# Convolution rows of the last group in five buffers stored from GpSimd's queue, sample loads behind head loads, softmax rows in other places

## The chip, the cores and the metric

The kernel runs on one core of a Trainium2 chip. The core has five engines, each with its own instruction order: TensorE (PE; PEld is its weight load), VectorE (DVE), ScalarE (ACT), GpSimd (POOL) and SyncE (SP). Here SP only issues DMAs, and GpSimd issues some beside its arithmetic. The metric is the device time of one execution in microseconds, as the median of several runs. Before the change it was 2948.85 us (three runs, 2946.77 to 2949.27).

## The reference

One layer of a streaming encoder for 2048 prompt frames and 8 samples of 16 new frames, all in fp32. What concerns this change is the first sub-layer, the mixer:

```
proj = rmsnorm(x) @ w_in               # -> q | k | v | u_val | u_gate
s    = q @ k^T / 8 + bias              # 8 heads of 64, each query sees 9 chunks of 64 keys
att  = softmax(s) @ v                  # samples: 256 cached keys and values and their own 16
u    = u_val * sigmoid(u_gate)
c    = silu(layernorm(causal_depthwise_conv(u, width 31)))
y    = concat(att, c) @ w_out
```

Cross-attention into 256 memory tokens and a SwiGLU layer follow; new key, value and convolution caches are outputs as well.

## The kernel before

The prompt is 16 tiles of 128 frames, and the samples together are a 17th tile (`S_TILE`). Every fp32 product is three matmuls of high and low parts (L283 to L285, L291). The phases follow each other: memory keys (`phase_mem`), the input projection with the convolution (`phase_proj`), attention, the output projection (`mixout`), cross-attention, SwiGLU.

`phase_proj` runs over three groups of six, six and five tiles. Per group it makes `u`, the values, then keys and queries, whose high and low parts go to DRAM (`ks`, `qs`, L714). The convolution of a group runs beside the projection on VectorE (L523) and GpSimd (L533). Its result `ct` is normalised by `conv_norm`, tile by tile: transposes (L538), statistics (L540), the normalised rows `xn` (L546), transposes back (L550), then on ScalarE `z` (L553, four activations) and its tanh (L556), on VectorE their product (L557), and a DMA that stores `z` into `cs[t]` (L558). For the first two groups this is spread over the next group. For the last group the five tiles' steps (`behind`, L731) stand between the last projections and attention. `z` has two buffers, and the store is issued by SP.

`attention` goes through 128 units (8 heads of 16 tiles). A unit makes scores (L865), a row minimum on VectorE (L802) and an exponential on ScalarE (L804) into a softmax row `z` (also so called, but another tag, with eight places); four units later come transposes (L882) and their split by a ScalarE cast (L883) and a VectorE subtraction (L884); every four units the value product (L895), a copy (L899) and a sum (L901). A head's keys, queries and values come back from DRAM by `head_load` (L789, L790) into two sets of buffers, during the head before; head 1's during the end of the projection. Beside head h runs `sample(h)`, whose loads are cached keys `kt` (L809), cached values `vc` (L811) and new values `vn` (L813); its scores are L825. The bias rows `bs` (L908) are loaded once.

`mixout` starts with the sample tile. It loads `cs[t]` (L1008) and splits it (L1023, L1024).

What sets the order: a scheduler places the recorded instructions on each engine in the order of their recording, except where one is free to go earlier; `issue_after(x)` keeps what is recorded under it behind `x`. Each engine runs its instructions strictly in that order. Buffers are places in a few large arenas (`sbF`, `fa`, `fb`, `sbR`; offsets in KB), given out in rotation by tag; an instruction waits for whoever used the same bytes before. `fb` from 0 holds `ct`; `fa` from 4 to 8 holds the two `z`.

Of the kernel before, what the change touches and what calls it, by code (L numbers as in the profile page):

```python
# [17 lines left out]
P = 128  # L18
# [118 lines left out]
class Build:  # L137
# [22 lines left out]
    def early(self, ctx):  # L160
# [15 lines left out]
                   .lay(sbR, 56, ("hhz", 8, 1), ("hlz", 8, 1))  # L176
                   .lay(sbR, 104, ("vv", 2, 2)))
        smp = Region().lay(fa, 28, ("qsamp", 2, 1), ("ksamp", 2, 1))
# [268 lines left out]
    def phase_proj(self):  # L447
# [87 lines left out]
        def conv_norm(t, cts, off, tag="tr"):  # L535
# [13 lines left out]
            for j in range(4):  # L549
                nc.tensor.transpose(pz[:, j, :], xn[:, j, :], self.ident[:, :])  # L550
            z = self.t(pool, [P, 4, P], F32, "z", 2)
            for j in range(4):
# [4 lines left out]
            nc.vector.scalar_tensor_tensor(z[:, :, :], th[:, :, :], 1.0, z[:, :, :], ALU.add, ALU.mult)  # L557
            nc.sync.dma_start(self.cs[t], z[:, :, :].rearrange("p a b -> p (a b)"))  # L558

# [17 lines left out]
        for gi, subs in enumerate(GROUPS):  # L577
# [100 lines left out]
            def qk(which, j, blk, x):  # L678
# [14 lines left out]
                else:  # L693
# [4 lines left out]
                    for i, t in enumerate(sub):  # L698
# [13 lines left out]
                        else:  # L712
                            nc.sync.dma_start(A["new_att_k_prompt"][(t - 12) * P:(t - 11) * P, :], kos[t][:, :])
                nc.sync.dma_start(dst[:, :, col:col + npc].rearrange("c p n -> p c n"),  # L714
                                  sp[:, :, :npc].bitcast(F32))

# [41 lines left out]
    def att_pools(self):  # L758
        sbF, sbR, fa, fb = self.sbF, self.sbR, self.fa, self.fb
        self.attp = (Region().lay(sbF, 34.5, ("kt", 4.25, 2), ("pp", 1.5, 1), ("vn", 2, 2))  # L760
                     .at("z", 2.5, (fa, [24]), (fb, [0, 2.5, 5]), (fa, [9, 11.5, 14, 16.5]))
                     .lay(fb, 7.5, ("vc", 4, 2), ("nmx", 0.03125, 12), ("sm", 0.03125, 2))
                     .lay(fa, 0, ("qbd", 0.5, 2), ("osb", 0.5, 2)).lay(fa, 5, ("otmp", 2, 1), ("bs", 1.0625, 1)).lay(fa, 19, ("bt", 2.5, 2))
                     .lay(sbR, 0, ("q20", 8, 1), ("k20", 8, 1), ("kl0", 8, 1), ("q21", 8, 1), ("k21", 8, 1), ("kl1", 8, 1),
                          ("v20", 8, 1), ("ph1", 10, 1), ("pl1", 10, 1), ("v21", 8, 1))
                     .lay(sbR, 88, ("ph0", 10, 1), ("pl0", 10, 1)))
# [12 lines left out]
    def head_load(self, h, tiles, a, b):  # L779


        nc = self.nc
        q2, k2, kl, v2, _ = tiles
        c = slice(a * P, b * P)
        rr = slice(h % 2 * DH, (h % 2 + 1) * DH)
        for o in range(2):
            half = slice(o * DH, (o + 1) * DH)
            for dst, src in ((k2, self.ks[h // 2][0]), (q2, self.qs[h // 2][o]), (kl, self.ks[h // 2][1])):
                nc.sync.dma_start(dst[half, c].bitcast(F32), src[rr, c])  # L789
        nc.sync.dma_start(v2[:, a:b, :].bitcast(F32), self.vs[h // 4][:, h % 4, a:b, :])  # L790

    def attention(self):
# [14 lines left out]
        def sample(s):  # L807
            kt = self.t(pool, [P, 4, PAST + DEC_S], F32, "kt", 2)
            nc.sync.dma_start(kt[:, :, :PAST], A["cache_att_kt"][s].rearrange("p (c k) -> p c k", k=PAST))  # L809
            vc = self.t(pool, [P, 2, 512], F32, "vc", 2)  # L810
            nc.sync.dma_start(vc[:, :, :], A["cache_att_v"][s].rearrange("(b p) d -> p b d", p=P))  # L811
            vn = self.t(pool, [DEC_S, 512], F32, "vn", 2)
            nc.sync.dma_start(vn[:, :], self.vsamp[s * DEC_S:(s + 1) * DEC_S, :])  # L813
            yield
# [105 lines left out]
        for i in range(n + LV + 1):  # L920
            if i < n:
# [3 lines left out]
                if t == 6 and h + 1 < H:  # L925
                    heads[h + 1] = self.head_tiles(h + 1)
                    self.head_load(h + 1, heads[h + 1], 0, NPT)
                zq[h, t] = scores(heads[h], t, self.sums[:, t, h:h + 1])
# [761 lines left out]
```

## Time and profile before

| | |
|---|---|
| median of three runs | 2948.85 us |
| the profiled execution | 2949.61 us, its span 2947.8 us |
| mean granted TensorE clock | 0.991 |
| busy shares | PE 97%, PEld 89%, DVE 71%, POOL 47%, ACT 44% |
| HBM | 366 MB read, 142 MB written |

Times in the profile are us from the span's start. A row of a timeline has start, length, engine, line, operation, output and input, count, and in brackets how long the engine stood idle before it and what ended that. A row of windows has a stretch, its length, the busy time of each engine with its instruction count, the granted TensorE clock as a share of full speed, the mean busy share of the 16 DMA engines, and GB/s. A row of waits has who waited for whom, us in total, times, the longest. "DMA to landing" is from issue to the arrival of all data. `flexb` is the tile name of both `fa` and `fb`, `psb` of PSUM.

### The profile page before, as it was taken

To read this page: it belongs to the slowest core of one execution; us is meant where nothing else is said; L and a number is where in the kernel's file an instruction comes from. 1 tells how busy PE (TensorE), PEld (TensorE's weight loads), DVE (VectorE), ACT (ScalarE), POOL (GpSimd) and SP (SyncE) were. 2 spreads that over 40 slices of the span, in tenths; PEclk is the share of its full clock that TensorE was granted. 3 is DMA by queue.
4 is the path that set the end of the run, shared out by engine and by line. 5 is a ranking of instruction groups with operands and counts; after the bars stand their busy time and mean duration, and the time that the engine had idled before them with its cause. 6 is when DMAs were issued, how large, how long until landed. Compare 5 with 4: busy or idle time off the path is not lost.

```text
span 2947.8 us, 45388 instructions
## 1 busy us (share of the span) xinstructions
PE 2872.6 (97%) x16740; PEld 2624.6 (89%) x16740; DVE 2079.8 (71%) x3024; ACT 1308.1 (44%) x2661; POOL 1371.4 (47%) x1247
## 2 busy tenths in 40 slices
PE   8999999979989999999999999999999999999998
PEld 8999999969978777888879999999999999888786
DVE  6697795969985336344469787788889997555655
ACT  4535364659874234232344333433344444333433
POOL 0268396730022224244557565465556775424413
PEclk9999999989999999999999999999999999999999
DMA  8735255558845665133355333644344446657754
GB/s 303 251 115 174 98 161 171 159 181 199 205 137 189 204 246 172 52 128 109 125 199 184 115 133 115 198 155 154 144 140 151 143 142 231 223 171 226 227 191 163
DMA packets 198474, 500.04 MB, mean 170 GB/s; under 512 B 18981, under 2 KB 87085, under 8 KB 189923
## 3 DMA queue, kind: packets, MB, share of 16 engines
q1 hardware_dynamic: 187931, 461.09, 48.4%
q0 software_dynamic: 10320, 36.05, 3.2%
q8 instruction: 131, 2.15, 0.3%
q14 instruction: 92, 0.75, 0.1%
HBM read 365.97 MB, written 141.81 MB: 172 GB/s over the span
## 4 chain that ended last, share of the span: by engine, by line
PE 43%; DMA 3%; POOL 2%; DVE 2%; issue 1%; ACT 0%; DVEq 0%; SPq 0%; POOLq 0%; ACTq 0%
PE psb L285 14%; PE psb L284 14%; PE psb L283 14%; PE psb L291 1%; DMA sbf<-in_w_down_dram 1%; DMA sbf<-x 1%; POOL sbf L1540 1%; PE psb L1395 1%; DMA sbf<-hn 1%; DVE sbr L1601 0%; POOL sbf L340 0%; DMA hn<-sbf 0%; DMA sbf<-in_w_gate_dram 0%; DVE flexb L1480 0%; DVE sbr L1418 0%
## 5 line engine op out<-in xcount | busy, mean ns | idle before, releaser
L283 PE MATMUL psb<-sbr 128*128 128x384 f32 (+3 forms) x2808 | 943.0, 337 | 3.7 <-ACT sbr L1600 1.5
L284 PE MATMUL psb<-sbr 128*128 128x384 f32 (+3 forms) x2356 | 806.1, 342 | 2.5 <-DVE sbr L320 2.4
L285 PE MATMUL psb<-sbr 128*128 128x512 f32 (+3 forms) x1848 | 633.9, 345 | 1.9 <-DVE sbr L1601 1.8
L283 PEld LDWEIGHTS psb<-sbr 128*128 128x128 f32 x2808 | 530.6, 189 | 33.6 <-ACT sbr L1600 2.6
L285 PE MATMUL psb<-sbr,sbx 128*128 128x384 f32 (+2 forms) x1484 | 476.7, 322 | 0.0
L284 PEld LDWEIGHTS psb<-sbr 128*128 128x128 f32 x2356 | 445.3, 189 | 29.5 <-DVE sbr L320 2.7
L285 PEld LDWEIGHTS psb<-sbr 128*128 128x128 f32 x1848 | 348.5, 189 | 31.4 <-DVE sbr L1601 4.6
L1418 DVE TENSOR_TENSOR sbr<-sbf,sbr 128x512 fp32r<-128x512 f32 x258 | 264.7, 1029 | 36.1 <-ACT sbr L1417 35.3
L1417 ACT CAST sbr<-sbf 128x512 fp32r<-128x512 f32 x258 | 159.4, 620 | 279.2 <-PE psb L284 231.4
L285 PEld LDWEIGHTS psb<-sbr,sbx 128*128 128x128 f32 x1484 | 280.5, 189 | 0.2
L523 DVE SCALAR_TENSOR_TENSOR psb<-sbf,psb 128x768 f32<-128x768 f32 (+1 forms) x290 | 264.2, 911 | 6.2
L291 PE MATMUL psb<-sbr 128*128 128x512 f32 x1004 | 247.3, 395 | 0.1
L1601 DVE TENSOR_TENSOR sbr<-sbf,sbr 128x384 fp32r<-128x384 f32 (+1 forms) x231 | 161.3, 721 | 94.3 <-ACT sbr L1600 93.4
L291 PEld LDWEIGHTS psb<-sbr 128*128 128x128 f32 x1004 | 185.8, 188 | 41.5 <-issue 2.5
L278 POOL TENSOR_TENSOR sbx<-sbf,sbr 128x1024 fp32r<-128x1024 f32 x60 | 152.9, 2550 | 81.2 <-ACT sbr L277 76.1
L1540 POOL TENSOR_TENSOR sbf<-sbf 128x512 f32<-128x512 f32 x77 | 106.2, 1385 | 169.2 <-DMA sbf<-in_w_down_dram 167.6
L1600 ACT CAST sbr<-sbf 128x384 fp32r<-128x384 f32 (+1 forms) x231 | 110.6, 497 | 165.2 <-PE psb L284 137.3
L533 POOL TENSOR_TENSOR flexb<-flexb,flexb 128x128 f32<-128x128 f32 (+1 forms) x180 | 167.4, 931 | 22.4 <-ACT flexb L532 12.9
L283 PE MATMUL psb<-sbr,sbx 128*128 128x384 f32 (+1 forms) x524 | 170.5, 327 | 1.2 <-ACT sbr L1397 0.7
L1417 ACT CAST sbx<-sbf 128x512 fp32r<-128x512 f32 x153 | 94.5, 620 | 160.9 <-PE psb L284 148.9
L291 PE MATMUL psb<-sbr,sbx 128*128 128x512 f32 x654 | 160.7, 397 | 4.1 <-ACT sbx L319 2.2
L1418 DVE TENSOR_TENSOR sbx<-sbf,sbx 128x512 fp32r<-128x512 f32 x153 | 152.4, 998 | 15.3 <-ACT sbx L1417 15.0
(328 smaller groups left out, 5938.8 us busy)
## 6 DMA issues: line engine op xcount, KB each, us to landing
af<-flexb SPq DMA_DIRECT2D x33, 1344.0 KB, 6.0
sbf<-in_w_down_dram SPq DMA_DIRECT2D x154, 256.0 KB, 3.7
sbf<-af SPq DMA_DIRECT2D x90, 384.0 KB, 4.2
sbf<-in_w_gate_dram SPq DMA_DIRECT2D x66, 512.0 KB, 3.3
sbf<-in_w_up_dram SPq DMA_DIRECT2D x66, 512.0 KB, 3.4
sbf<-x SPq DMA_DIRECT2D x50, 512.0 KB, 3.8
sbf<-in_w_in_dram SPq DMA_DIRECT2D x48, 512.0 KB, 3.9
sbr<-ks SPq DMA_DIRECT2D x28, 512.0 KB, 9.6
```

Of the source, the lines that this page charges most:

```text
L278: self.lo_engine.tensor_tensor(lo[:, :], wf[:, :], hi[:, :].bitcast(F32), ALU.subtract)
L283: nc.tensor.matmul(ps, lh, rh, start=start, stop=False, **kw)
L284: nc.tensor.matmul(ps, lh, rl, start=False, stop=False, **kw)
L285: self.last_product = nc.tensor.matmul(ps, ll, rh, start=False, stop=stop, **kw)
L291: self.last_half = nc.tensor.matmul(y[o], l, r[:, o * 512:(o + 1) * 512], start=start and x == 0, stop=stop and x == 2)
L523: nc.vector.scalar_tensor_tensor(acc if w < CW - 1 else o, src(w), cwt[:, j, w:w + 1], acc, ALU.mult, ALU.add)
L533: nc.gpsimd.tensor_tensor(o, o, v, ALU.add)
L1417: nc.scalar.copy(hs[j][:, :], src[j])
L1418: nc.vector.tensor_tensor(ls[j][:, :], src[j], hs[j][:, :].bitcast(F32), ALU.subtract)
L1540: nc.gpsimd.tensor_tensor(acc[:, :], acc[:, :], q[:, :], ALU.add if s > 0 else ALU.subtract)
L1600: nc.scalar.copy(ch[:, m], a[:, x, m])
L1601: nc.vector.tensor_tensor(cl[:, m], a[:, x, m], ch[:, m].bitcast(F32), ALU.subtract)
```

## The change

Four edits. `z` of the last group gets a tag of its own, `zx`, with five places: the two old ones in `fa`, and three in `sbF` where the weight buffers and later the attention output lie. Its stores are issued by GpSimd. The three loads of `sample(h)` are kept behind the last load recorded before: the value load of head h, or for sample 0 the last store of queries. And the eight places of the softmax rows come in another order, so that three in `fa` are used before those in `fb`.

```diff
-                   .lay(sbR, 104, ("vv", 2, 2)))
+                   .lay(sbR, 104, ("vv", 2, 2)).at("zx", 2, (fa, [4, 6]), (sbF, [8, 10, 6])))
...
-            z = self.t(pool, [P, 4, P], F32, "z", 2)
+            z = self.t(pool, [P, 4, P], F32, "z" if tag == "tr" else "zx", 2)
...
-            nc.sync.dma_start(self.cs[t], z[:, :, :].rearrange("p a b -> p (a b)"))
+            (nc.sync if tag == "tr" else nc.gpsimd).dma_start(self.cs[t], z[:, :, :].rearrange("p a b -> p (a b)"))
...
-                nc.sync.dma_start(dst[:, :, col:col + npc].rearrange("c p n -> p c n"),
-                                  sp[:, :, :npc].bitcast(F32))
+                self.last_load = nc.sync.dma_start(dst[:, :, col:col + npc].rearrange("c p n -> p c n"),
+                                                   sp[:, :, :npc].bitcast(F32))
...
-                     .at("z", 2.5, (fa, [24]), (fb, [0, 2.5, 5]), (fa, [9, 11.5, 14, 16.5]))
+                     .at("z", 2.5, (fa, [24, 11.5, 14, 16.5]), (fb, [0, 2.5, 5]), (fa, [9]))
...
-        nc.sync.dma_start(v2[:, a:b, :].bitcast(F32), self.vs[h // 4][:, h % 4, a:b, :])
+        return nc.sync.dma_start(v2[:, a:b, :].bitcast(F32), self.vs[h // 4][:, h % 4, a:b, :])
...
             kt = self.t(pool, [P, 4, PAST + DEC_S], F32, "kt", 2)
-            nc.sync.dma_start(kt[:, :, :PAST], A["cache_att_kt"][s].rearrange("p (c k) -> p c k", k=PAST))
             vc = self.t(pool, [P, 2, 512], F32, "vc", 2)
-            nc.sync.dma_start(vc[:, :, :], A["cache_att_v"][s].rearrange("(b p) d -> p b d", p=P))
             vn = self.t(pool, [DEC_S, 512], F32, "vn", 2)
-            nc.sync.dma_start(vn[:, :], self.vsamp[s * DEC_S:(s + 1) * DEC_S, :])
+            with self.tc.issue_after(self.last_load.ins):
+                nc.sync.dma_start(kt[:, :, :PAST], A["cache_att_kt"][s].rearrange("p (c k) -> p c k", k=PAST))
+                nc.sync.dma_start(vc[:, :, :], A["cache_att_v"][s].rearrange("(b p) d -> p b d", p=P))
+                nc.sync.dma_start(vn[:, :], self.vsamp[s * DEC_S:(s + 1) * DEC_S, :])
...
-                    self.head_load(h + 1, heads[h + 1], 0, NPT)
+                    self.last_load = self.head_load(h + 1, heads[h + 1], 0, NPT)
```

From `sample` on, line numbers of the changed kernel are one higher (L825 becomes L826, and so on).

ScalarE at the handoff from projection to attention. `flexb_153` is `fa`, `flexb_157` is `fb`; a wait on `DMAHW` is one for a DMA from SP. Before:

```order
L804 ACTIVATE flexb_153,sbf<-flexb_153,flexb_157 128x640 [waits DVE_49]
L883 CAST sbx<-psb 128x384 [waits DVE_49,PE_49]
L553 ACTIVATE flexb_153<-psb,sbf 128x128 [waits DMAHW0_49]
L553 ACTIVATE flexb_153<-psb,sbf 128x128 x3
L553 ACTIVATE flexb_153<-psb,sbf 128x128 [waits DMAHW2_49]
L553 ACTIVATE flexb_153<-psb,sbf 128x128
L556 ACTIVATE flexb_153<-flexb_153 128x512 [waits Activation_49]
L553 ACTIVATE flexb_153<-psb,sbf 128x128 x2
L556 ACTIVATE flexb_153<-flexb_153 128x512 [waits DVE_49,Activation_49]
L883 CAST sbx<-psb 128x256 [waits PE_49]
L553 ACTIVATE flexb_153<-psb,sbf 128x128 [waits DMAHW4_49]
L553 ACTIVATE flexb_153<-psb,sbf 128x128 x3
```

And after:

```order
L804 ACTIVATE flexb_157,sbf<-flexb_157 128x640 [waits DVE_49]
L553 ACTIVATE sbf<-psb,sbf 128x128 [waits PE_49]
L553 ACTIVATE sbf<-psb,sbf 128x128 x3
L556 ACTIVATE flexb_153<-flexb_153 128x512 [waits DVE_49]
L553 ACTIVATE sbf<-psb,sbf 128x128 [waits PE_49]
L553 ACTIVATE sbf<-psb,sbf 128x128 x3
L804 ACTIVATE flexb_157,sbf<-flexb_157 128x640 [waits DVE_49]
L804 ACTIVATE flexb_157,sbf<-flexb_157 128x640 [waits DVE_49,Pool_49]
L556 ACTIVATE flexb_153<-sbf 128x512 [waits DVE_49]
L553 ACTIVATE sbf<-psb,sbf 128x128 [waits PE_49]
L553 ACTIVATE sbf<-psb,sbf 128x128 x3
L884 CAST sbx<-psb 128x384 [waits PE_49]
```

The third, fourth and fifth tile's L553 wait for TensorE instead of a DMA, and two more exponentials (L804) stand ahead of the cast of 384 columns.

TensorE at the same place, around sample 0's scores (L825, then L826). Before:

```order
L882 MATMUL psb<-ident_73,flexb_157 128x128 [waits DVE_49]
L882 MATMUL psb<-ident_73,flexb_157 128x128 x2
L550 MATMUL psb<-ident_73,flexb_153 128x128 [waits Activation_49]
L550 MATMUL psb<-ident_73,flexb_153 128x128 x3
L825 MATMUL psb<-sbf,flexb_153 32x272 [waits DMAHW7_49,DVE_49,Pool_49]
L825 MATMUL psb<-sbf,flexb_153 32x272 x3
L882 MATMUL psb<-ident_73,flexb_157 128x128 [waits Activation_49]
L882 MATMUL psb<-ident_73,flexb_157 128x128
L882 MATMUL psb<-ident_73,flexb_153 128x128 [waits Activation_49]
```

And after:

```order
L866 MATMUL psb<-sbr 128x384 [waits DVE_49]
L866 MATMUL psb<-sbr 128x384
L866 MATMUL psb<-sbr 128x256 x2
L550 MATMUL psb<-ident_73,flexb_153 128x128 [waits DVE_49,Activation_49]
L550 MATMUL psb<-ident_73,flexb_153 128x128 x3
L883 MATMUL psb<-ident_73,flexb_153 128x128 x3
L883 MATMUL psb<-ident_73,flexb_153 128x128 [waits Activation_49]
L883 MATMUL psb<-ident_73,flexb_153 128x128
L826 MATMUL psb<-sbf,flexb_153 32x272 [waits DMAHW5_49,DVE_49,Pool_49]
L826 MATMUL psb<-sbf,flexb_153 32x272 x3
L883 MATMUL psb<-ident_73,flexb_153 128x128 [waits Activation_49]
```

The scores still follow the fifth tile's transposes (L550), but more head scores (L866) and transposes come ahead of them, and the DMA that they wait for is now the load further down in SP's order.

SP, from the end of the projection. Before:

```order
L714 DMA qs_12_84<-sbf 128x2x384 [waits DMAHW5_49,DVE_49]
L714 DMA qs_12_84<-sbf 128x2x128 [waits DMAHW6_49,DVE_49]
L714 DMA ks_17_89<-sbf 128x2x384 [waits DMAHW7_49,DVE_49]
L809 DMA sbf<-in_cache_att_kt_dram 128x4x256 [waits DMAHW0_49,DVE_49,PE_49]
L789 DMA sbr<-qs_10_82 64x2048 [waits DMAHW1_49,PE_49]
L789 DMA sbr<-qs_10_82 64x2048 [waits DMAHW2_49]
L789 DMA sbr<-ks_14_86 64x2048 [waits DMAHW3_49,PE_49]
L713 DMA out_dram<-sbf 128x512 [waits DMAHW4_49,Activation_49]
L713 DMA out_dram<-sbf 128x512 [waits DMAHW5_49,Activation_49]
L714 DMA qs_13_85<-sbf 128x2x384 [waits DMAHW6_49,DVE_49]
L789 DMA sbr<-ks_14_86 64x2048 [waits DMAHW7_49]
```

And after, from the last of head 1's keys on:

```order
L789 DMA sbr<-ks_14_86 64x2048 [waits DMAHW6_49]
L714 DMA ks_17_89<-sbf 128x2x128 [waits DMAHW7_49,DVE_49]
L790 DMA sbr<-vs_18_90 128x2048 [waits DMAHW0_49,PE_49,Pool_49]
L812 DMA sbf<-in_cache_att_kt_dram 128x4x256 [waits DMAHW1_49]
L814 DMA sbf<-vsampd_149 16x512 [waits DMAHW2_49]
L714 DMA qs_13_85<-sbf 128x2x128 [waits DMAHW3_49,DVE_49]
L713 DMA out_dram<-sbf 128x512 [waits DMAHW4_49,Activation_49]
L812 DMA sbf<-in_cache_att_kt_dram 128x4x256 [waits DMAHW5_49]
L813 DMA flexb_157<-in_cache_att_v_dram 128x2x512 [waits DMAHW6_49,PE_49]
L711 DMA out_dram<-sbf 8x16x512 [waits DMAHW7_49,Activation_49]
L814 DMA sbf<-vsampd_149 16x512 [waits DMAHW0_49]
L813 DMA flexb_157<-in_cache_att_v_dram 128x2x512 [waits DMAHW1_49,DVE_49,PE_49]
```

Sample 1's `kt` stood ahead of head 1's first load and sample 0's far above; now both stand behind head 1's values, sample 0's after the last store of queries. The five L558 are gone from SP. On GpSimd the first is placed ahead of the fifth tile's reciprocal root:

```order
L298 TENSOR_SCALAR flexb_157<-flexb_157 128x1 [waits DVE_49]
L301 TENSOR_TENSOR flexb_157<-flexb_157,mhalf_78 128x1 [waits Pool_49]
L558 DMA cs_32_104<-flexb_153 128x512 [waits DVE_49]
L298 TENSOR_SCALAR flexb_157<-flexb_157 128x1 [waits DVE_49]
L301 TENSOR_TENSOR flexb_157<-flexb_157,mhalf_78 128x1 [waits Pool_49]
L913 MEMSET flexb_153 128x128 [waits DMAHW5_49,PE_49]
L558 DMA cs_33_105<-flexb_153 128x512 [waits DVE_49]
L913 MEMSET flexb_153 128x128 [waits PE_49]
L558 DMA cs_34_106<-sbf 128x512 [waits DVE_49]
L816 COPY sbf<-flexb_153 128x4x16 [waits PE_49]
L558 DMA cs_35_107<-sbf 128x512 [waits DVE_49]
L558 DMA cs_36_108<-sbf 128x512 [waits DVE_49]
```

Before, GpSimd had the same rows without the five L558.

## The prediction

> **What bounds the kernel now.** I read the page first, then the stages by windows, then the waits of the one stage that stands out, then the timelines of its engines.
>
> ```profile
> PE 2872.6 (97%) x16740; PEld 2624.6 (89%) x16740; DVE 2079.8 (71%) x3024; ACT 1308.1 (44%) x2661; POOL 1371.4 (47%) x1247
> ```
>
> ```profile
> core 0: us, PE busy (x) PEld busy (x) DVE busy (x) ACT busy (x) POOL busy (x), PEclk, DMA share, GB/s
> ...
> 630.00:640.00 10.00, 4.31 (x19) 2.61 (x17) 5.41 (x12) 4.62 (x13) 1.13 (x2) 0.67 1.01 282
> 640.00:650.00 10.00, 2.94 (x14) 1.23 (x14) 2.84 (x9) 4.53 (x11) 0.88 (x3) 0.50 0.65 239
> ...
> 626.00:664.00 38.00, 21.00 (x112) 15.51 (x110) 20.88 (x50) 23.16 (x61) 4.57 (x10) 0.69 0.67 210
> 664.00:826.00 162.00, 161.84 (x1284) 147.88 (x1282) 149.88 (x365) 146.84 (x352) 7.77 (x22) 1.00 0.86 208
> ```
>
> TensorE is busy 97% of the span, so a change that moves no matmul can win only where TensorE stands still. The windows show the largest such place: at the handoff from projection to attention TensorE is busy for 4.31 and 2.94 us of two stretches of 10. The last row is attention running undisturbed: TensorE's modelled busy time is full, but VectorE (149.88 of 162, 92.5%) and ScalarE (146.84, 90.6%) have little left either. Had 626 to 664 run at those shares, VectorE would have done 35.2 us of work there and did 20.88, ScalarE 34.4 and did 23.16. So the whole handoff holds 14.3/0.925 = 15 us by VectorE and 11.2/0.906 = 12.4 us by ScalarE: no version of this stage gains more.
>
> ```profile
> PE psb L550 <- ACT flexb L553: 8.2, 1, 8.2
> PE psb L882 <- ACT flexb L553: 3.6, 2, 3.1
> ...
> ACT flexb L553 <- DMA cs<-flexb: 8.2, 3, 6.2
> ```
>
> ```profile
> 626.43 2.89 ACT L553 ACTIVATE flexb<-psb,sbf 128x128 f32<-128x128 f32 x8
> 630.64 0.28 ACT L688 ACTIVATE sbf<-psb 128x128 fp32r<-128x128 f32 x1 [1.33 <-DMA qs<-sbf]
> ...
> 635.34 0.83 ACT L804 ACTIVATE flexb<-flexb,flexb 128x640 f32<-128x640 f32 x1 [1.05 <-DVE flexb L802]
> ...
> 637.02 0.48 ACT L883 CAST sbx<-psb 128x384 fp32r<-128x384 f32 x1 [0.77 <-PE psb L882]
> ...
> 646.79 0.62 ACT L556 ACTIVATE flexb<-flexb 128x512 f32<-128x512 f32 x1
> ...
> 648.89 0.37 ACT L883 CAST sbx<-psb 128x256 fp32r<-128x256 f32 x1
> ...
> 652.44 0.26 ACT L883 CAST sbx<-psb 128x128 fp32r<-128x128 f32 x1
> ...
> 655.12 0.56 ACT L883 CAST sbx<-psb 128x512 fp32r<-128x512 f32 x1
> ...
> 662.57 0.82 ACT L804 ACTIVATE flexb<-flexb 128x640 f32<-128x640 f32 x1
> 663.29 0.20 ACT L804 ACTIVATION_READ_ACCUMULATOR flexb<-flexb 128x1 f32 x1
> ```
>
> TensorE waits 11.8 us for L553, ScalarE's writing of the convolution rows `z`. ScalarE itself waits before L553 three times, 8.2 us in all, for the stores of earlier rows, since five tiles share two buffers; attention's casts (L883) and exponentials (L804) stand behind it in ScalarE's order. Why the stores are late:
>
> ```profile
> 616.37 0.57 SPq L809 DMA_DIRECT2D sbf<-in_cache_att_kt_dram  x1
> 617.37 1.12 SPq L789 DMA_DIRECT2D sbr<-qs  x2
> ...
> 630.06 0.59 SPq L811 DMA_DIRECT2D flexb<-in_cache_att_v_dram  x1
> ...
> 635.11 0.32 SPq L558 DMA_DIRECT2D cs<-flexb  x1
> ```
>
> ```profile
> L558 SPq DMA_DIRECT2D cs<-flexb x1: 319/319/319, 635.1 to 635.1; - x1
> ...
> DMA to landing us min/median/max: 8.5/8.5/8.5
> ```
>
> ```profile
> L811 SPq DMA_DIRECT2D flexb<-in_cache_att_v_dram x1: 587/587/587, 630.1 to 630.1; - x1
> ...
> DMA to landing us min/median/max: 11.9/11.9/11.9
> ```
>
> The first store is issued at 635.11 and lands 8.5 us later, at 643.6, because SP has put head 1's loads ahead of it; sample 0's cached values, issued at 630.06, land at 642.0. The windows show 282 and 239 GB/s there, with all DMA engines busy.
>
> **The change, part by part.**
>
> *Five buffers.* No row of L553 waits for a store any more; ScalarE can run through. I replay its new order (front part) with durations from the rows above: four L553 1.45 (half of 2.89), L556 0.62, an exponential with its read 1.02 (0.82 + 0.20; those of 384 and 512 columns, scaled by width, 0.7 and 0.9), casts of 384, 256 and 128 columns 0.48, 0.37, 0.26. From 626.43: one tile's L553 to 627.9. Then L688, which waited until 630.64 for a store of `qs` and now stands one tile earlier; with sample 1's keys (512 KB) gone from ahead of that store I take 628.6. L688 and L553 to 630.3, L556, two copies and the two short exponentials to 633.2, tile 4's exponential 634.2, L553 635.6, L556 and L553 637.7, two exponentials 639.7, L556 and the last L553 641.7, casts of 384 and 256 columns and L556 643.1. There the cast of 128 columns follows; before it stood at 652.44, and two exponentials fewer had been done.
>
> *Sample loads queued behind the head's.* That cast needs transposes which TensorE now has behind L825, sample 0's scores. Before, those keys were loaded ahead of this stage; now they go after head 1's whole load and after sample 1's keys. This is the new wait. Its size: up to the store of 635.11 SP's queue held everything that will now stand ahead of sample 0's keys, but for sample 0's values (512 KB), which now follow. Take those and the 256 KB store out, put the keys (512 KB) and the first store from GpSimd's queue (256 KB) in: the same bytes, so the keys land where that store did, 643.6. A second GpSimd store, issued later than the keys, adds 256 KB, 1 us, and I count half: 644.2. Bounds: 642 (the landing of the transfer that leaves) and 649 (7.5 MB, all that goes through the keys, from 617.4 at 239 GB/s).
>
> ```profile
> 646.54 1.13 PE L825 MATMUL psb<-sbf,flexb 128*32 128x272 f32 x8 [0.21 <-issue]
> ...
> 653.51 1.12 PE L882 MATMUL psb<-ident,flexb 128*128 128x128 f32 x4 [1.11 <-DVE sbx L884]
> 654.28 1.42 PE L865 MATMUL psb<-sbr 128*128 128x384 f32 x4
> ```
>
> ```profile
> 620.00:622.00 2.00, 2.00 (x19) 2.00 (x18) 1.24 (x4) 0.41 (x2) 0.64 (x3) 1.00 0.98 205
> 656.00:658.00 2.00, 2.00 (x13) 1.85 (x11) 1.96 (x5) 1.41 (x3) 0.00 (x0) 0.69 0.18 37
> ```
>
> From 644.2 at half clock: L825 1.13, one transpose, so the 128-column cast ends at 646.1; exponential 647.1, L556 647.7, two 512-column casts (0.56 each, with short gaps) 649.2 (TensorE's scores, 1.42, and transposes are done by then), exponential 650.2, two casts 651.3, exponential of tile 9 at 652.3, copy of the first values (0.6, taken like a cast of that width) 652.9, a cast 653.5, the sample's exponential 0.7: 654.2. Before, the same work ended with tile 9's exponential at 663.29 + 0.20 = 663.5. **Gain 9.3 us.** If the keys came by 642, ScalarE would not stop: 12.0. If at 649: 4.5.
>
> The clock: TensorE restarts at 653.5 at half clock (0.50 in 640 to 650) and is on its way to the full one in 656 to 658 (mean 0.69). I give the new restart the same, since the new wait is of the same kind and 5 us long.
>
> *Stores from GpSimd's queue.* SP loses five issues. GpSimd takes five, like these of a later stage:
>
> ```profile
> L1076 POOL DMA_DIRECT2D x<-flexb x17: 573/628/680, 907.4 to 1158.1; - x17
> ...
> DMA to landing us min/median/max: 2.9/5.0/9.8
> ```
>
> 5 x 0.63 = 3.1 us on an engine busy 4.57 of 38: hidden. Queued behind them there are the fills of `qbd` and the copies into `kt` (L815), needed only by L825, which waits for its keys anyway. Landing 2.9 to 9.8 us after an issue at about 633 and 638 means 648 at the latest; the first writer of those places, the copy of values, comes at 652.3. The cover is 4 us; beyond it the loss is one for one. [...] No row here shows a GpSimd store beside a full SP queue. [...]
>
> *In later heads* sample loads come after the head's values, a head ahead of their use, and TensorE does not stand still between 664 and 826 (161.84 busy of 162). Nothing, bounds -1 to +1. SP's shorter waits there buy nothing for the same reason.
>
> *Places reordered.* At the start it lets the second to fourth rows lie away from the convolution's `ct`: part of the replay. At the end the last row now lies where tile 0's convolution rows load (L1008).
>
> ```profile
> 885.26 0.33 SPq L1008 DMA_DIRECT2D flexb<-cs  x1
> 889.24 0.62 ACT L1023 CAST sbx<-flexb 128x512 fp32r<-128x512 f32 x1
> 890.04 0.60 PE L882 MATMUL psb<-ident,flexb 128*128 128x128 f32 x4
> 895.53 1.05 ACT L277 CAST sbr<-sbf 128x1024 fp32r<-128x1024 f32 x1 [4.26 <-PE psb L895]
> ```
>
> ```profile
> flexb<-cs SPq DMA_DIRECT2D x15, 256.0 KB, 4.8
> ```
>
> The load moves from 885.26 to the end of the last transposes, 890.6. With 4.8 us to land ScalarE's cast moves from 889.24 to 895.4; ScalarE was idle until 895.53. Cost 0 to 1, I take 0.5.
>
> **Sum.** 9.3 - 0.5 = 8.8. The profiled execution took 2949.61 (span 2947.8 and 1.8 around it), 0.8 above the median 2948.85 of the runs. 2949.6 - 8.8 = 2940.8; from the median 2940.05. I say 2940.5.
>
> **Rivals.** *Keys in time* (12 - 0.5): 2937. For it: ScalarE reaches the cast only at 643.1, 1 us before my landing. Against: the two landings shown took 8.5 and 11.9 us. *The gain mostly eaten* (keys or stores 3 to 9 us later): 2944 to 2949, within 0.2%, which is 5.9 us and about what a measurement can tell from no change. For it: stores, keys and values of both samples now crowd into the same 15 us. *Slower:* sample 0's keys. TensorE runs in order, so all attention waits at L825. The gain is gone when L825 starts at 653.5, where TensorE restarted before. The 7.5 MB through the keys, from 617.4 at the 205 GB/s of 620 to 622, land at 654.0, and with all of the third GpSimd store ahead (0.26 MB) at 655.3: L825 1.8 us late, and 2951.9 with the 0.5 of the end. Against it: the rows of 630 to 650 show 282 and 239 GB/s. *The change doesn't do what it says:* the order shows no store among L553's waits, so only the cause of the wait could be wrong; ScalarE's rows name the stores, 8.2 us. Inside "mostly eaten".
>
> **Chances.** Forecast (gain 6 to 11) 0.52, keys in time 0.18, mostly eaten 0.21, slower 0.09. So faster 0.70, same 0.21, slower 0.09. Range: 2935 (upper rival and 2 for the 12.4 us limit) to 2948 leaves out the slower case and a little of either end. The likeliest alone: 2938 to 2943.
>
> **What the profile will show.** L553 waits for no DMA; TensorE waits ahead of L825 for some 5 us until 643 to 645, at half clock; ScalarE runs nearly unbroken from 629 to 643; the exponential of tile 9 ends near 652.3; the stretch 664 to 826 is the same but earlier; the end of attention keeps its order. I am wrong if L825 waits past 650, if L899 waits for GpSimd's stores, or if attention's later stages stretch by what the handoff gave.

## The result, and the profile after

| | before | after |
|---|---|---|
| median of 22 runs each | 2949.14 us | 2944.28 us |
| ratio, 95% interval | | 0.9981 (0.9976 to 0.9987) |
| the profiled execution | 2949.61 us | 2946.83 us |

The change makes the kernel 5.6 us faster by the ratio (3.8 to 7.1), 4.9 by the medians: about the 0.2% that the prediction set as the border between "same" and "faster". The forecast was 2940.5, within 2935 to 2948; the direction was right, the size, 8.8, was 1.6 to 1.8 times too large. The median lies just inside the rival "mostly eaten" (2944 to 2949), and a gain of 4.9 to 5.6 just outside the forecast's 6 to 11, though the keys came as forecast and not 3 to 9 us later; a second measurement, 2942.31 (8.0 us by its ratio), lies within the likeliest case. The profiled execution lies 2.6 us above its median.

First the line of busy times of the page after, then the waits of TensorE from 612 to 690 us, then of ScalarE (who waited for whom, us in total, times, longest).

```profile
PE 2871.7 (98%) x16740; PEld 2623.9 (89%) x16740; DVE 2083.8 (71%) x3024; ACT 1308.8 (44%) x2661; POOL 1375.9 (47%) x1252
```

```profile
PE psb L866 <- DVE flexb L802: 5.2, 6, 1.0
PE psb L826 <- DMA sbf<-in_cache_att_kt_dram: 4.5, 1, 4.5
```

```profile
ACT flexb L804 <- DVE flexb L802: 5.2, 7, 2.4
ACT sbx L884 <- PE psb L883: 4.8, 3, 4.2
```

The waits for stores are gone: TensorE's 11.8 us for L553 and ScalarE's 8.2. In their place stands the new wait, 4.5 us of L826 for sample 0's keys. In the timelines after, SP's queue issues those keys at 633.25, TensorE starts on them at 643.63, and ScalarE, which had caught up at 640.21 + 0.75, stands still until the cast behind them, at 645.21:

```profile
633.25 0.58 SPq L812 DMA_DIRECT2D sbf<-in_cache_att_kt_dram  x1
```

```profile
643.63 1.13 PE L826 MATMUL psb<-sbf,flexb 128*32 128x272 f32 x8 [4.55 <-DMA sbf<-in_cache_att_kt_dram]
...
654.79 0.61 PE L866 MATMUL psb<-sbr 128*128 128x384 f32 x2 [0.98 <-DVE flexb L802]
656.42 1.43 PE L866 MATMUL psb<-sbr 128*128 128x384 f32 x4 [1.02 <-DVE flexb L802]
...
659.88 0.65 PE L845 MATMUL psb<-flexb,sbf 128*32 128x128 f32 x16
```

```profile
640.21 0.75 ACT L556 ACTIVATE flexb<-sbf 128x512 f32<-128x512 f32 x1
645.21 0.27 ACT L884 CAST sbx<-psb 128x128 fp32r<-128x128 f32 x1 [4.24 <-PE psb L883]
...
655.26 0.19 ACT L804 ACTIVATION_READ_ACCUMULATOR flexb<-flexb,flexb 128x1 f32 x1
656.40 0.83 ACT L804 ACTIVATE flexb<-flexb,flexb 128x640 f32<-128x640 f32 x1 [0.96 <-DVE flexb L802]
658.53 0.37 ACT L837 COPY sbf<-psb 128x256 f32<-128x256 f32 x1 [1.21 <-PE psb L835]
```

To compare kernels I use one number, the loss of a stage: the time in which TensorE stands still, and half of the time in which it is busy at half clock (there matmuls take up to nearly twice as long: L826's eight take 1.13 us at half clock, at 643.63 in the changed kernel, and 0.67 at full, at 675.01; the half is thus an estimate, rather too large). But for the matmuls added in two experiments, TensorE's work is the same in all kernels, so what one loses less than another it is faster by. The windows give it. Before, after, and for a later experiment with sample 0's loads free ("free0"), for the handoff (612 to 690), the middle of attention and its end (820 to 900):

```profile
612.00:690.00 78.00, 61.00 (x424) 53.28 (x422) 54.02 (x131) 50.44 (x131) 7.95 (x20) 0.85 0.71 194
690.00:820.00 130.00, 129.84 (x1035) 118.33 (x1034) 120.24 (x290) 117.77 (x283) 6.27 (x18) 1.00 0.87 209
820.00:900.00 80.00, 71.95 (x485) 62.06 (x484) 61.91 (x135) 55.80 (x125) 19.73 (x13) 0.96 0.39 130
```

```profile
612.00:690.00 78.00, 66.04 (x470) 58.53 (x469) 56.93 (x137) 55.45 (x143) 10.38 (x25) 0.91 0.73 207
690.00:820.00 130.00, 129.64 (x1013) 118.19 (x1012) 120.00 (x292) 117.20 (x282) 6.28 (x18) 1.00 0.85 209
820.00:900.00 80.00, 73.51 (x484) 62.76 (x483) 63.93 (x129) 53.85 (x118) 24.43 (x17) 0.98 0.42 144
```

```profile
612.00:690.00 78.00, 70.85 (x519) 62.54 (x518) 62.39 (x154) 60.98 (x158) 10.36 (x25) 0.96 0.78 216
...
820.00:900.00 80.00, 73.91 (x463) 62.36 (x456) 60.38 (x118) 48.60 (x107) 24.66 (x20) 0.98 0.41 140
```

Handoff: TensorE stands still 17.0 us before (78 - 61.00) and 12.0 after; of its busy time 9.8 and 11.2 us run at half clock (by the granted clock: 24 us at half before, in one piece; after in three pieces, 13.7 together). Loss 21.9 before, 17.5 after: 4.3 us won. End of attention: 10.5 and 8.0, 2.5 won. The middle loses 0.2 and 0.4. Together 6.8, or 6.6 with the middle, which agrees with the ratio. The profiled pair differs by only 2.8, because this execution loses 3.4 us more than the one of before behind 900 us, in stages that the change doesn't touch (31.4 and 28.0, up to 15 us ahead of the span's end); a second profile of the same kernel (below) loses 27.1 there.

### The profile page after: what moved, and what is told of

Read it like the earlier page. It is cut to its first block, busy times and chain, and to the rows that moved or that the text cites. A ratio compares the mean times of both kernels' runs of the same rounds, so it can differ in the third digit from the quotient of the medians.

```text
span 2945.0 us, 45369 instructions
## 1 busy us (share of the span) xinstructions
PE 2871.7 (98%) x16740; PEld 2623.9 (89%) x16740; DVE 2083.8 (71%) x3024; ACT 1308.8 (44%) x2661; POOL 1375.9 (47%) x1252
## 4 chain that ended last, share of the span: by engine, by line
PE 41%; DMA 4%; POOL 3%; DVE 2%; issue 1%; ACT 0%; DVEq 0%; SPq 0%; POOLq 0%; ACTq 0%
PE psb L285 13%; PE psb L283 13%; PE psb L284 13%; PE psb L291 1%; DMA sbf<-x 1%; DMA sbf<-in_w_down_dram 1%; POOL sbf L1541 1%; DMA sbf<-hn 1%; PE psb L1396 1%; DMA sbf<-in_w_gate_dram 0%; DVE sbr L1419 0%; POOL sbf L340 0%; DMA out_dram<-sbf 0%; DVE sbr L1602 0%; DMA hn<-sbf 0%
## 5 line engine op out<-in xcount | busy, mean ns | idle before, releaser
L291 PE MATMUL psb<-sbr 128*128 128x512 f32 x1004 | 247.3, 395 | 0.1
L1602 DVE TENSOR_TENSOR sbr<-sbf,sbr 128x384 fp32r<-128x384 f32 (+1 forms) x231 | 171.1, 763 | 94.6 <-ACT sbr L1601 93.7
L291 PEld LDWEIGHTS psb<-sbr 128*128 128x128 f32 x1004 | 185.9, 188 | 41.5 <-issue 2.5
L291 PE MATMUL psb<-sbr,sbx 128*128 128x512 f32 x654 | 160.9, 397 | 3.7 <-ACT sbx L319 2.2
```

The lines of the kernel that those rows point to most:

```text
L291: self.last_half = nc.tensor.matmul(y[o], l, r[:, o * 512:(o + 1) * 512], start=start and x == 0, stop=stop and x == 2)
L1602: nc.vector.tensor_tensor(cl[:, m], a[:, x, m], ch[:, m].bitcast(F32), ALU.subtract)
```

## The experiments

Each was timed beside the kernel before, whose median on those chips was 2950.3 to 2951.6. "Loss" is the sum just defined, from each run's own profile, one execution each.

| run | median us | ratio (95%) | loss at handoff | at the end |
|---|---|---|---|---|
| before | 2949.1 to 2951.6 | 1 | 21.9 | 10.5 |
| loads | 2949.16 | 0.9993 (0.9983 to 1.0003) | 22.0 | 9.3 |
| buffers | 2948.57 | 0.9992 (0.9983 to 1.0001) | 17.0 | 10.8 |
| noloads | 2945.54 | 0.9983 (0.9974 to 0.9992) | 13.7 | 10.1 |
| hold1 | 2945.24 | 0.9978 (0.9968 to 0.9987) | 12.8 | 11.9 |
| oldplaces | 2942.84 | 0.9980 (0.9970 to 0.9990) | 17.7 | 9.3 |
| again (the changed kernel) | 2942.31 | 0.9973 (0.9962 to 0.9983) | 18.5 | 8.2 |
| warm | 2946.84 | 0.9990 (0.9981 to 0.9999) | 20.4 | 10.5 |
| warm2 | 2945.39 | 0.9979 (0.9970 to 0.9988) | 14.5 | 8.7 |
| free0_old | 2943.45 | 0.9972 (0.9960 to 0.9983) | 16.6 | 8.0 |
| free0_sp | 2940.79 | 0.9968 (0.9957 to 0.9980) | 15.0 | 8.3 |
| free0 | 2935.62 | 0.9950 (0.9937 to 0.9964) | 10.6 | 7.7 |
| free0_b (the same) | 2937.74 | 0.9957 (0.9945 to 0.9970) | 11.2 | 7.9 |

In warm and warm2 the matmuls added count as idle time. The two losses together, against before's 32.4, agree with the time by the ratio within 3 us in each run but noloads (8.6 less loss, 5.0 us faster; its profiled execution was the fastest of its eleven runs).

**The changed kernel again** (no edit).

> The changed kernel once more, for a second profile. Theory A (the gain is made at the handoff and kept): ratio 0.998, TensorE 4.5 to 5 us ahead of the kernel before from 680 us on, as in the first profile. Theory B (much of the 4.9 us is made elsewhere, at the end of the projection and at the end of attention, and differs from execution to execution): the lead at 680 us is again some 4 to 5 us, but the steps of 1.0 us near 500 us and of 2.3 us near 830 to 880 us are not there again, or others are.

Measured: the handoff wins 3.4 and the end 2.3, as in the first profile (4.3 and 2.5). L826 waits only 2.5 us, but the clock is at half for 20.5 us in one piece, and 3.4 more later (mean 0.85 over 612 to 690, against 0.91). So the two parts are there each time; the clock at the handoff is what varies. Theory A holds for the ratio and fails on the lead: some 2.5 us ahead at 680 us, not 4.5, since this execution had lost 1.6 us more than before already ahead of 600.

**Sample 0's loads free** (free0), and once more on another chip (free0_b).

```diff
-            with self.tc.issue_after(self.last_load.ins):
+            with self.tc.issue_after(self.last_load.ins) if s else ExitStack():
```

> The changed kernel, but sample 0's three loads may go as early as they did before; those of samples 1 to 7 stay behind their head's loads. Theory A (the wait for sample 0's keys at L826 costs the difference between the 9.3 us of the forecast and the 12.0 of keys in time): TensorE does not wait at L826, and the kernel is 2.7 us faster than the changed one. Theory B (past 650 us attention's own chain of scores, row minimum, exponential and transposes at a low clock sets the time, whatever ScalarE has gained): the wait of 4.5 us at L826 goes and comes back as waits for L802 and L804; within 1 us of the changed kernel.

> The version with sample 0's loads free once more, on another chip, for a second profile and a second ratio. Theory A (the wait for the keys costs 6.7 us): ratio 0.995 within 0.0015, loss at the handoff 10 to 12 us against 17.5 to 18.5 of the changed kernel. Theory B (the first measurement was luck of the clock): ratio near 0.9975.

Measured: 6.7 us faster than the changed kernel on the same chip, by ratio 0.23%; on the other chip 0.9957. SP's timeline shows sample 0's keys issued at 586.66, TensorE's has its scores at 637.56 with no wait ahead of them:

```profile
586.66 0.61 SPq L812 DMA_DIRECT2D sbf<-in_cache_att_kt_dram  x1
```

```profile
637.56 1.10 PE L826 MATMUL psb<-sbf,flexb 128*32 128x272 f32 x8
```

The rows of windows above show where the time is: TensorE stands still 7.15 us instead of 11.96, and 6.8 us of clock at half instead of 13.7. Loss 10.6 instead of 17.5. So the edit is worth 7.0 here, with a wait of 4.5 gone: 4.8 less standing still, and 2.2 for the two half-clock windows more (a window is 3.4 us; last section). Against the second profile of the changed kernel (18.5, a wait of 2.5) it is worth 7.9: 2.6 and 5.4. Both are far above the 2.7 of Theory A, which had the cause but not the price. Theory B (it comes back as other waits) falls: the wait for L802 is 4.8 us in six pieces, 5.2 in the changed kernel. This is the version that beats both kernels.

**No sample load held** (noloads: buffers, stores and places alone) and **sample 1's held alone** (hold1).

```diff
 noloads, against the changed kernel
-            with self.tc.issue_after(self.last_load.ins):
 hold1, against the changed kernel
-            with self.tc.issue_after(self.last_load.ins):
+            with self.tc.issue_after(self.last_load.ins) if s == 1 else ExitStack():
```

> Five buffers, stores from GpSimd's queue and new places, but no sample load is held behind a head's loads. Theory A: the new wait at L826 was the price of that edit, so without it 2.7 us faster than the changed kernel; head 1's loads come later by sample 1's 512 KB, which nobody waits for. Theory B: the same time within 1 us. A third possibility: sample loads of 2 MB ahead of head loads make a later head's first scores wait, and the kernel is 2 us or more slower than the changed one.

> Only sample 1's loads are held behind head 1's; those of sample 0 and of samples 2 to 7 are free. Theory A (what held loads win is in two places: at the handoff through sample 1's 512 KB ahead of head 1's loads, and at the end of attention, where the output weights land 1.5 us sooner): handoff as with sample 0 free, loss 10 to 12 us, end of attention as before with a wait of 1.6 us of L835; 2 to 3 us slower than with all of samples 1 to 7 held. Theory B (all of it is at the handoff): the same time within 1 us.

Measured: noloads 9.9 us slower than free0 on the same chip, hold1 7.5, though sample 0's scores wait for no load in either. noloads lost 3.1 us more at the handoff in its profile, hold1 2.2 (it stands still no longer, 7.5 us, but has 13.7 us at half clock in one piece, a mean of 0.91 over 612 to 690, where free0 has 0.96), and at the end they lost 2.4 and 4.2 more. That is the third possibility of noloads by its size, but no later head's first scores wait. At the end TensorE's transposes of sample 7's row wait for GpSimd, 1.7 us in noloads and 1.5 in hold1, where sample 7's loads are free (waits from 690 to 900 us, noloads, then after):

```profile
PE psb L834 <- POOL flexb L829: 1.7, 1, 1.7
```

```profile
PE psb L835 <- POOL flexb L830: 0.2, 1, 0.2
```

GpSimd multiplies that row (L829) behind a cast of the first output weights (L277), which SP loads (L273). SP and GpSimd in noloads, then after:

```profile
801.75 0.53 SPq L811 DMA_DIRECT2D flexb<-in_cache_att_v_dram  x1
...
811.50 0.34 SPq L273 DMA_DIRECT2D sbf<-in_w_out_dram  x1
```

```profile
819.62 1.04 POOL L277 CAST sbr<-sbf 128x1024 fp32r<-128x1024 f32 x1 [8.28 <-DMA sbf<-in_w_out_dram]
```

```profile
814.23 0.34 SPq L273 DMA_DIRECT2D sbf<-in_w_out_dram  x1
...
819.40 0.60 SPq L812 DMA_DIRECT2D sbf<-in_cache_att_kt_dram  x1
```

```profile
820.82 1.04 POOL L277 CAST sbr<-sbf 128x1024 fp32r<-128x1024 f32 x1 [7.35 <-PE psb L883]
```

In noloads the weights go out behind sample 7's values (L811), and the cast waits for them until 8.1 us after their issue; after, that sample's loads come behind the weights, and the cast starts after 6.6 us and waits for something else last. Before the change it was as in noloads: 819.00 to 827.05, and a wait of 1.6 us at L834. After the change the wait is 0.2 us, and the clock is at half near 865 us for one window of 3.4 us instead of two. All four kernels with these loads free wait 1.5 to 1.9 us there. Of those with held loads warm waits 1.2 (its cast started 7.6 us after the issue, and its end lost 10.5, as before), the others 0.6 at most. So holding the loads is the likely cause of the gain at the end, as Theory A of hold1 said, but it doesn't fix the size: loads and oldplaces hardly wait and still have two half-clock windows, and win only 1.2. Of noloads' 9.9 us, 5.5 are seen against free0's profile, of hold1's 7.5 (2 to 3 were expected), 6.4; why their handoffs lose more than free0's, and where the rest of the 9.9 is, stays open, since one execution of each was profiled.

**Old places** in the changed kernel (oldplaces) and with sample 0's loads free (free0_old).

```diff
-                     .at("z", 2.5, (fa, [24, 11.5, 14, 16.5]), (fb, [0, 2.5, 5]), (fa, [9]))
+                     .at("z", 2.5, (fa, [24]), (fb, [0, 2.5, 5]), (fa, [9, 11.5, 14, 16.5]))
```

> The changed kernel with the eight softmax places in the old order. Theory A (the exponentials of tiles 1 to 3 are held back by the places under the convolution rows): ScalarE has less to do ahead of 640 us and the same exponentials after L826, some 2 to 3 us slower than the changed kernel at the handoff, 0.5 us won back at the end of attention. Theory B (ScalarE does not set the time past 650 us): within 1 us of the changed kernel.

> Sample 0's loads free and the softmax places in the old order. Theory A (the new order of places is worth 3 us once nobody waits for the keys, as between the run of buffers alone and the one without held loads, 2948.6 and 2945.5, and worth nothing while the wait at L826 covers it): 2 to 4 us slower than with the new places, TensorE waiting some 4 us for L802 between 640 and 660 us. Theory B (the order of places is worth nothing anywhere): the same time within 1 us.

Measured: 2942.84 against 2942.31 for the changed kernel on one chip, no difference clear of noise; 2943.45 against 2937.74 with sample 0's loads free, 5.7 us slower (4.4 by the ratios), more than expected. TensorE's waits, oldplaces, then free0_old:

```profile
PE psb L826 <- DMA sbf<-in_cache_att_kt_dram: 6.6, 1, 6.6
PE psb L866 <- DVE flexb L802: 1.5, 3, 0.9
```

```profile
PE psb L866 <- DVE flexb L802: 5.0, 3, 3.7
```

In oldplaces TensorE comes to sample 0's scores earlier and waits 6.6 us there instead of 4.5, but 1.5 for L802 instead of 5.2: what the places hold back is hidden by the wait for the keys. Without that wait it stands in the open, 3.7 us in one piece.

**The stores on SP**, with sample 0's loads free (free0_sp).

```diff
-            (nc.sync if tag == "tr" else nc.gpsimd).dma_start(self.cs[t], ...
+            nc.sync.dma_start(self.cs[t], ...
```

> The version with sample 0's loads free, but the last group's rows are stored by SP as before. Theory A (the buffers do the work and nobody waits for a store): the same time as that version within 1 us. Theory B (on SP the issue of a store waits for its rows and holds back all loads behind it, head 1's or the samples'): waits for a load between 640 and 690 us, 2 us or more slower than that version.

Measured: slower than free0 by 0.0011 to 0.0018 of the time, 3 to 5 us, with intervals that overlap; nearer Theory B, but by another way. The bias rows of the samples (L909, `bs`) are loaded into `fa` from 7 to 8, which is part of the second tile's row (`zx` from 6 to 8), so they wait until that row's store has landed. That landing ends SP's long wait ahead of them in both versions (waits of SP from 630 to 655 us, free0, then free0_sp):

```profile
SPq L909 <- DMA cs<-flexb: 6.9, 1, 6.9
```

```profile
SPq L909 <- DMA cs<-flexb: 1.4, 1, 1.4
```

VectorE's minimum for sample 0 waits for the bias rows, and TensorE for VectorE. SP and TensorE in free0_sp:

```profile
642.60 4.21 SPq L558 DMA_DIRECT2D cs<-sbf  x3
648.24 3.56 SPq L909 DMA_DIRECT2D flexb<-toep  x8
```

```profile
653.41 0.44 DVE L802 CUSTOM_DVE_ANT_0 flexb<-psb,flexb 128x272 f32<-128x272 f32 x1 [1.79 <-DMA flexb<-toep]
```

```profile
653.91 1.01 PE L866 MATMUL psb<-sbr 128*128 128x384 f32 x2 [2.67 <-DVE flexb L802]
```

On SP the second store goes out at 642.19, 2.6 us after its row is done (638.92 + 0.68, L557): in SP's order a load of values (L813) goes first, at 640.53. GpSimd issues it 0.3 us after (636.22; 635.22 + 0.68). On SP it lands after 6.0 us, at 648.19. The three held stores of the row above are out by 646.81, before that. In free0 the bias rows were issued at 642.98, but this execution is 3.5 us late already at sample 0's scores (641.04 against 637.56), so the 5.3 us between are not the store's alone: counted from the end of the second row the bias rows leave after 8.6 us here and 7.1 in free0, 1.6 later. TensorE's wait of 2.67 is 0.65 in free0; of the 4.4 us more loss, 2.2 are standing still and 2.2 half clock. So GpSimd's queue is worth something for the second store, whose place the bias rows need; how much of the 3 to 5 us that is stays open.

**The buffers and GpSimd's stores alone** (buffers) and **the held loads alone** (loads), each over the kernel before.

```diff
 buffers
+    ... .at("zx", 2, (fa, [4, 6]), (sbF, [8, 10, 6])))
+            (nc.sync if tag == "tr" else nc.gpsimd).dma_start(self.cs[t], ...
 loads
+            with self.tc.issue_after(self.last_load.ins):
```

> Five buffers and their stores from GpSimd's queue alone, over the kernel before: sample loads unheld, softmax places in the old order. Theory A (sample 0's keys are the price): no wait at L825, so at least as much won at the handoff as by the whole change, 5 us or more faster than before. Theory B (all parts are needed): the exponentials of tiles 1 to 3 stay behind the convolution rows' places and TensorE waits for them; 2 to 4 us faster.

> The sample loads held behind head loads alone, over the kernel before (two buffers, stores by SP, old places). Theory A: L553 still waits some 6 to 8 us for stores, which now have the keys and values of both samples near them, and L826 comes behind that anyway; handoff 0 to 2 us slower than before. At the end of attention the weights of the output projection land 1.5 us sooner after their issue, as in the changed kernel, and L835's wait of 1.6 us goes: together the same as before within 2 us. Theory B (held loads disturb later heads): 3 us or more slower, with waits between 680 and 820 us.

Measured: buffers 2.4 us faster by the ratio (-0.3 to 5.0), nearer Theory B. L553 waits for nothing, but TensorE waits 5.7 us for L802, 4.4 in one piece, for the old places; the loss at the end is before's. Loads: no difference that can be measured, as Theory A said; TensorE waits 9.4 us at once for L553, and the loss is before's at the handoff and 1.2 less at the end. Neither alone brings more than 2.4 us by the ratio (5.0 at the end of the interval); buffers, places and held loads together with early keys for sample 0 bring 13 to 15.

**More matmuls during the wait** (warm, warm2).

```diff
+                q2, k2 = heads[0][:2]
+                for _ in range(24):
+                    nc.tensor.matmul(two[:, 1, :], q2[:, :P], k2[:, :512], start=True, stop=True)
```

> The changed kernel with 24 more matmuls of 128x512 ahead of sample 0's scores, on operands that are there already and into the unused half of the scores' place, so that TensorE works while it waits for the keys; they take about 5 us at full clock. Theory A (the wait of 4.5 us costs 7 because TensorE restarts at half the clock after it): the keys land as before at 643 to 645, the granted clock is full or back sooner, and the kernel is 1 to 2.5 us faster than the changed one. Theory B (the clock is not what the wait costs): the same time, or slower by what the added matmuls take past the keys' landing, 1 to 5 us.

Measured: 2946.84. The added matmuls (L829; L826 is L831 here) did not stand where they were meant: their operands were ready, so the scheduler put 22 of them at 632.79, ahead of the last tiles' transposes, 6.88 us (the 5 us expected for 24 were an estimate; 1004 of that size take 247.3 us in the page before, L291, so 5.9 for 24), and L831 still waited 4.7 us. The run tells nothing of the clock. In warm2 they read sample 0's queries instead:

```diff
+                for c in [0, 1, 2, 3] * 5:
+                    nc.tensor.matmul(two[c * 32:(c + 1) * 32, 1, :n], qb[:, c, :], old, start=True, stop=True)
```

> As the run with added matmuls, but they now read sample 0's queries, which are ready only at 638 us, so that they stand directly ahead of sample 0's scores: 20 matmuls of 32x272 on four column groups, 5 times 0.67 = 3.4 us at full clock, 5.7 at half (as L826's own took). Theory A (the clock at the restart is a third of what the wait costs): TensorE is busy during most of the wait of 4.5 us, the granted clock stays or is back at full within 645 us, the loss at the handoff (idle time and half of the busy time at half clock, the added work counted as idle) falls by 1 to 2.5 us. Theory B (the clock follows more than these few us): half clock past 645 as in the changed kernel, no gain or a loss up to 3 us.

```profile
645.17 3.06 PE L829 MATMUL psb<-flexb 128*32 128x272 f32 x40
648.26 0.65 PE L831 MATMUL psb<-sbf,flexb 128*32 128x272 f32 x2
```

```profile
646.00:648.00 2.00, 2.00 (x36) 0.92 (x28) 1.50 (x3) 1.24 (x4) 0.63 (x2) 0.91 1.08 401
648.00:650.00 2.00, 1.97 (x15) 0.74 (x12) 0.79 (x3) 0.55 (x2) 0.61 (x2) 1.00 1.04 387
```

Now TensorE is busy through the wait, the clock is full when the scores start (0.91 and 1.00, where the changed kernel had 0.50), and the loss at the handoff, the added work counted as idle, is 14.5, 3 to 4 less than in the changed kernel. But the ratio, 0.9979, is the changed kernel's. The profile speaks for Theory A, the times for neither; that the clock at this restart is worth time was not shown by this run.

## Why the prediction was right, and where it was not

*Five buffers: right.* No L553 waits for a store, ScalarE runs without a gap through 630 to 640 us (busy 2.00 us of every 2).

*Sample loads queued: the landing right, its price mis-sized.* Said: keys land at 644.2, TensorE waits some 5 us at half clock. Measured: L826 at 643.63, 4.55 us. But the prediction took 9.3 us for the gain with this wait and 12.0 without it, 2.7 for the wait. The 12.0 is near what free0 wins at the handoff, 11.3 and 10.7 (noloads and hold1, which don't wait for keys either, win 8.2 and 9.1). Holding sample 0's loads costs 7.0 and 7.9, and the term "Gain 9.3" measured 4.3 and 3.4. Two steps failed. The wait was priced by how long ScalarE would stand still, from 643.1 on; ScalarE was there at 641.0 and could not use its lead. And the gain was read off at ScalarE's exponentials, though TensorE's order sets the end. At the sample's exponential ScalarE is 8.0 us earlier than before (655.45 against the 663.5 of the prediction), where 9.3 was forecast; then it waits 0.96 for VectorE and 1.21 for TensorE (rows above), which waits 0.98 and 1.02 itself and runs at half clock again (0.51 from 656.20 to 659.60). At the sample's value product TensorE is 4.2 us earlier: 659.88, and before:

```profile
664.12 0.65 PE L844 MATMUL psb<-flexb,sbf 128*32 128x128 f32 x16
```

*The clock: wrong.* "I give the new restart the same": the restart got 6.8 us at half clock, a later 3.4 more, and 20.5 in one piece in the second profile.

*Stores from GpSimd's queue: hidden, but the cover was misread.* The prediction took the copy of values for the first writer of the stored rows' places. It is the load of the bias rows, which waited 2.4 us for the second store, hidden because VectorE held it up 5.7 us more, to 649.09. Once the keys are early, that store ends the wait (6.9 us in free0). The second store, issued at 637.7, landed after 5.7 us, at 643.4, with the keys that SP had issued 4.4 us ahead of it and that landed after 10.2. The prediction had no row of a GpSimd store beside a full SP queue; this is one.

*Later heads: right* (690 to 820 us lose 0.2 and 0.4), but the end of attention belongs to them and won 2.5 us: the loads of the last sample made way for the output weights, the likely cause (noloads).

*Places: the load of tile 0's rows moved as said and cost nothing.* ScalarE waits 2.76 us for it, and TensorE not at all:

```profile
886.88 0.62 ACT L1024 CAST sbx<-flexb 128x512 fp32r<-128x512 f32 x1 [2.76 <-DMA flexb<-cs]
```

*The sum.* Said 9.3 - 0.5 = 8.8; measured 4.3 + 2.5 = 6.8 in the first profile, 3.4 + 2.3 = 5.7 in the second, 5.6 and 8.0 by the two ratios. An error of 5 to 6 us at the handoff was half made up by one of 3 at the end, a gain that the prediction didn't know of: that the total came so near is in part luck.

*Two slips that change nothing above.* 14.3/0.925 is 15.5, not 15, and the limit by ScalarE, 12.4, is the tighter one. Of the rows of 630 to 650 us only the first shows all DMA engines busy (share 1.01); the second has 0.65.

## What to carry to other kernels

When a change takes a wait from one engine and gives the next in-order engine a new one, price the new wait on the engine whose order sets the end, at its full length, and add what the clock takes at the restart (2.2 and 5.4 us of the 7.0 and 7.9 here); a lead that another engine gains meanwhile need not last: ScalarE's 8.0 us here were 4.2 on TensorE 4 us later. Before loads are queued behind others, look which of them is used first: holding the loads of seven samples gained (free0 against noloads), holding those whose keys were needed first cost 7 us. Take a stage's edits apart and put them together: new places were worth nothing that could be measured while the wait for the keys covered them, and 4.4 to 5.7 us once it was gone. And when a buffer is stored by another queue, look for every later tenant of its bytes: the copy of values was not the first.

## What the clock did

In the profiles of before and after the granted clock of TensorE is either full or half, and its stretches at half between 600 and 900 us are 23.89 and 6.83 us long before, 3.41, 6.83, 3.41 and 3.41 after: one, two and seven times 3.41. Windows of that grid in the changed kernel (the columns are those of the windows above; the first number is TensorE's busy time, the clock stands behind GpSimd's):

```profile
632.30:635.70 3.40, 1.47 (x10) 1.06 (x8) 1.79 (x6) 3.40 (x10) 0.79 (x2) 0.99 1.07 289
635.70:639.10 3.40, 3.36 (x13) 2.96 (x13) 2.17 (x7) 3.40 (x10) 1.06 (x3) 0.50 1.00 388
639.10:642.50 3.40, 0.00 (x0) 0.00 (x0) 0.58 (x1) 1.86 (x5) 0.54 (x1) 1.00 1.09 390
642.50:645.90 3.40, 1.54 (x9) 0.41 (x9) 1.01 (x3) 0.27 (x1) 0.26 (x1) 0.50 1.04 400
645.90:649.30 3.40, 3.15 (x13) 3.15 (x14) 3.37 (x10) 2.14 (x4) 0.54 (x1) 0.50 0.31 119
649.30:652.80 3.50, 3.47 (x24) 3.10 (x23) 2.92 (x6) 3.25 (x7) 0.54 (x1) 1.00 0.41 133
652.80:656.20 3.40, 1.44 (x8) 0.72 (x6) 2.76 (x7) 1.84 (x5) 0.45 (x1) 0.99 0.26 87
```

In these rows a window's clock goes with the work of the one before it: 1.47 us of work in 3.4, and the next is at half; 3.36, and the next is at full. In the profiles of before and after, on this grid between 600 and 900 us, each of the six drops came after a window in which TensorE was busy for 0 to 51% of the time, each of the six returns after one of 88% or more. After 53% (from 628.84 in after) and 65% (from 827.90 in before) it stayed full, after 70% (from 633.34 in before) it stayed at half. I had not expected the drop at 635.7: in the window ahead of it TensorE had two gaps, 1.03 and 0.93 us, and no longer one. That may also be why executions of one kernel differ here, which no run shows by itself: a window that was 51% busy was followed by a drop and one that was 53% busy was not, and the handoff had 13.7 us at half clock in one profile of the changed kernel and 23.9 in the other.
